# Four of nine parts of a wide projection as block products in a stage of their own

## The chip, the cores and the metric

One core of a Trainium2 chip runs the kernel. The metric is the device time of one execution in microseconds (us); the time of a kernel is the median of several runs. TensorE (PE) multiplies matrices into PSUM; VectorE (DVE), ScalarE (ACT) and GpSimd (POOL) work on data in SBUF, the first two in PSUM too; SyncE (SP) issues most of the transfers.

## The reference: what is computed

One step of a decoder layer for 1024 prompt rows and 8 x 4 sample rows, so T = 1056 rows of 1024 numbers in fp32. Shortened:

```
z = rmsnorm(x, norm_mix_g)
h, c, b, u, v, q, gA, gB, gM = split(z @ w_in)          # nine parts of 1024 columns
y_a = b * causal_dwconv3(c * h)
y_b = u * spatial_gate(layernorm(v))                    # chunks of 128 rows
y_m = softmax(q k_mem^T / 16) v_mem                     # 4 heads, 256 memory rows
x = x + (sig(gA)*y_a + sig(gB)*y_b + sig(gM)*y_m) @ w_o
[a, g] = causal_dwconv3(rmsnorm(x) @ w_up) + bias       # 2 x 2816 columns
y = rmsnorm(x + (silu(g) * a) @ w_down)
```

The prompt attends to memory keys and values that are computed here; each of the 8 sample groups attends to a cache of its own. Outputs are y, the last rows of both convolutions, the memory keys and values, and the normalised v of the sample rows.

## The kernel before

Numbers are held transposed: a tile has 128 of the 1024 features on its partitions and the 1056 rows along it. Every fp32 operand is split into a high part (a rounded copy, on ACT) and a low part (the rest, on DVE or POOL), and every product is three matmuls: high x high, high x low, low x high (`three`, lines 210 to 213). zhi and zlo hold the two parts of the normalised input; S (8 tiles) holds sums.

**Units, chunks and slots.** A unit is one tile of 128 output columns of a weight: 512 KB are loaded by SP into a ring of three buffers (`load_unit`, L166), split into wh and wl (`split_unit`, L188 and L190) up to two units ahead, and used by `main` in three chunks of 352 rows. A chunk is 24 matmuls of 352 columns into one of three PSUM banks ("mm"), and then its evacuation. Side work lies as closures in the list `aux`; `weave` is called twice in each chunk (a slot, half a chunk), and spreads the list evenly over the slots that `pace(n)` announced; `drain` issues what is left. All engines work in the order in which this program issues, each in its own queue.

**Stages.** The part v (24 units) with the norm of x; the memory keys and values; then four heads h of attention, each with 16 units: q (two tiles), h, c, b, h, c, b, u, u, gB, gB, gA, gA, gM, gM. Then w_o, the up projection, the down projection. The first head's evacuations begin at about 190 us, the last gM's are at about 1013; the up projection begins at about 1113.

**A head's side work** (`att_items`, 83 items, and 4 for transposing cached rows) begins behind the two q units and is paced over 62 slots. Item 0 (`rows`) writes the sample rows' q to DRAM; `fetch_q` reads it back spread over all partitions, 512 KB each of eight times; `fetch` loads the sample groups' keys. `product(bb, mt)`, 16 items, is four DVE instructions each (L844), the sample rows' scores. `kv_load` and `kv_split` (ACT, then DVE at L960) bring the prompt's keys and values in two parts; `kv_split` stands between the products of bb = 6 and bb = 7. Then come, interleaved, `score(i)` (12 matmuls, maximum at L978, exponentials at L981, scaling at L988), `turn_p(i)` (transposes of the result and its two parts) and `value(i)` (12 matmuls), i from 0 to 3; then the sample rows' softmax, the values' fetches, their two parts (`parts`) and their matmuls (`against`).

**Evacuations.** q on ACT and DVE (two parts); u multiplies S on DVE (L1125); gB: sigmoid on ACT (L1130) into one of two tiles `sig`, a multiplication into S on DVE (L1136); gA and gM: sigmoid, then two DVE operations (L1143, L1144); h a copy; c a product and the three taps of the convolution (L305, L307); b a product. The last gM also makes zhi and zlo of S for w_o, and S is then loaded anew with x from DRAM.

**Block products.** The up projection already uses Winograd's form of Strassen's scheme: for two tiles of columns (a pair), the input is cut into 2 x 2 blocks of (4 feature tiles) x (two quarters of 264 rows), and seven products in the order 1, 2, 6, 5, 7, 3, 4 replace eight. Sums of input blocks are made once (`norm2`, L1245 to L1250), sums of weight blocks for each pair on POOL (L1361 to L1363, L1384), each sum gets its two parts (L1380, L1381) four products ahead, and the results are added on DVE into a scratch tile and the outputs (`evacuate`, L1477; L1479 on ACT). A product is 24 matmuls of 264 columns into one of three pairs of PSUM banks. The taps of the convolution follow on DVE (L1436, L1440), and the gate's multiplication on POOL (L1453).

**Buffers.** 9 slots for fp32 (`fs`) and 8 for the rounded type (`rs`), each 128 x 1088, are handed out first in, first out.

Of the kernel before, what the change touches and what calls it, by code (L numbers as in the profile page):

```python
# [15 lines left out]
P = 128  # L16
# [41 lines left out]
def layer_step(ctx: ExitStack, tc: tile.TileContext, I, O):  # L58
# [83 lines left out]
    for h in range(4):  # L142
        f0, f1 = 2 * h, 2 * h + 1
        seq = [("q", f0), ("q", f1)]
        for f in (f0, f1):
            seq += [("h", f), ("c", f), ("b", f)]
        for n in ("u", "gB", "gA", "gM"):
            seq += [(n, f0), (n, f1)]
        plan.append(seq)
        for n, f in seq:  # L150
            if (n, f) == ("gM", 7):
                for x in range(4, 8):
                    unit_cols(w_o, x * P, hold=True)
            unit_cols(w_in, COLS[n] + f * P)
    for f in range(8):
        unit_cols(w_o, f % 4 * P)
# [20 lines left out]
    def split_unit(eng=nc.vector):  # L177
        i = state["split"]
        if i < len(units):
            _, nk, cols, hold = units[i]  # L180
            t = stage.pop(i)
            if hold:
                kept[i] = rs.get(), rs.get()
# [4 lines left out]
            nc.scalar.copy(out=hi, in_=t)  # L188
            split_lows()
            lows.append(lambda: eng.tensor_tensor(out=lo, in0=t, in1=f32(hi), op=ALU.subtract))  # L190
            split[i] = (hi, lo)
            state["split"] += 1
# [163 lines left out]
    with tc.manual_schedule():  # L356
        slots = ctx.enter_context(tc.tile_pool(name="slots", bufs=1))
        fs = Slots(slots, [f"fs{i}" for i in range(9)], F32)
        rs = Slots(slots, [f"rs{i}" for i in range(8)], F32R)
# [133 lines left out]
        mh = [rs.get(), rs.get()]  # L493
        ml = [rs.get(), rs.get()]
# [16 lines left out]
        wt = rs.get()  # L511
# [87 lines left out]
        def sgu_norm(j):  # L599
# [13 lines left out]
            def go_n():  # L613
# [14 lines left out]
                for half in range(2):  # L628
                    fr = slice(half * 512, (half + 1) * 512)
                    p = rs.get()  # L630
# [14 lines left out]
        def sgu_mix(j, g):  # L645
            def go():
# [19 lines left out]
                if g % 2:  # L666
                    rs.put(sg.pop(("p", j, g // 2)))
            return go

        def sgu_done():  # L670
            rs.put(wt)
# [134 lines left out]
        rs.put(*mh, *ml)  # L806
# [6 lines left out]
        def att_items(h):  # L813
            qh, ql = att["q"]
            att["ym"] = ym = [None, None]
# [4 lines left out]
            def rows():  # L820
# [3 lines left out]
                att["qr"] = qr = small.tile([P, 256], F32, name="qr", tag="qr", bufs=1)  # L824
                nc.scalar.copy(out=qr[:32], in_=b[:32, :256])
                nc.scalar.dma_start(out=q_d[h], in_=qr[:32])
# [10 lines left out]
            def product(bb, mt):  # L837

                def go():
                    t = v3(att["st", bb // 2], 4, 256)  # L840
                    q = v3(att["qb", bb], 4, 256)
                    for i in range(4):
                        at = 4 * bb + i
                        nc.vector.tensor_tensor_reduce(  # L844
                            out=att["qr"], in0=q[:, i, :], in1=t[:, 2 * (bb % 2) + mt, :], scale=1.0, scalar=0.0,
                            op0=ALU.mult, op1=ALU.add, accum_out=att["sc"][:, mt, at : at + 1],
                        )
                    if mt:
                        fs.put(att.pop(("qb", bb)))
                        if bb % 2:  # L850
                            fs.put(att.pop(("st", bb // 2)))
                return go
# [16 lines left out]
            def masked():  # L869
                att["m"] = [rs.get(), rs.get()]  # L870
# [13 lines left out]
            def parts(i, e):  # L884
                def go():
                    t = att["st", i][:, e * 512 : (e + 1) * 512]
                    k = rs.get()
# [7 lines left out]
            def against(bb):  # L895
                def go():
# [12 lines left out]
                    rs.put(k)  # L909
# [23 lines left out]
            def folded_o():  # L933
# [10 lines left out]
                rs.put(*att.pop("m"))  # L944
# [11 lines left out]
            def kv_split():  # L956
                t = att.pop("kvs")
                hi, lo = rs.get(), rs.get()
# [5 lines left out]
            def score(i):  # L964
                def go():
# [23 lines left out]
                    att["p", i] = p  # L989
                return go  # L990

            def turn_p(i):
                def go():
# [9 lines left out]
                    t = rs.get()  # L1003
# [5 lines left out]
            def value(i):  # L1009
                def go():  # L1010
# [10 lines left out]
                    rs.put(t)  # L1021
                    for dt in range(2):
                        nc.scalar.copy(out=ym[dt][:, i * 256 : (i + 1) * 256], in_=b[:, dt * 256 : (dt + 1) * 256])
                    if i == 3:
                        rs.put(*att.pop("kv"))
# [26 lines left out]
        wo, back = {}, set()  # L1052
        pr = O["new_conv_a_prompt"][0, 0]
        sa = O["new_conv_a_sample"][0].rearrange("b k c -> (b k) c")

        def wo_take(f):
            def go():
                wo[f] = next_unit()
                ahead()
# [3 lines left out]
        def wo_ready(c):  # L1063
            def x_back():
                back.add(c)
                for fr in (slice(0, 4), slice(4, 8)):
                    nc.scalar.dma_start(out=S[:, fr, c * CH : (c + 1) * CH], in_=xT_d[c, :, fr, :])

            aux.extend([lambda: None] * 2 + [x_back])
            pace(3)  # L1070
            if c == 2:
                aux.extend(lambda i=i: tail_rows(tail_a[i // 4], i, 4, pr, sa) for i in (0, 4))
                pace(6)

        for h in range(4):
            qh, ql = [rs.get(), rs.get()], [rs.get(), rs.get()]
            hold = {}
            att["qs"] = small.tile([P, 2, 32], F32, name="qs", tag="qs", bufs=2)

            def q_evac(f):  # L1080
                dc = f % 2

                def go(c, r, ps):
                    if c == 2:
                        nc.scalar.mul(out=att["qs"][:, dc, :], in_=ps[:, CH - 32 :], mul=0.0625)
                    nc.scalar.mul(out=qh[dc][:, r], in_=ps, mul=0.0625)
                    nc.vector.scalar_tensor_tensor(
                        out=ql[dc][:, r], in0=ps, scalar=0.0625, in1=f32(qh[dc][:, r]), op0=ALU.mult, op1=ALU.subtract
                    )
                return go  # L1090

            def h_evac(f):
                hold["h", f] = fs.get()

                def go(c, r, ps):
                    nc.scalar.copy(out=hold["h", f][:, r], in_=ps)
                return go

            def c_evac(f):
                hb, hf = fs.get(), hold["h", f]  # L1100
                halo(hb, hal_a[:, f, :])

                def go(c, r, ps):
                    srcs = hb_parts(c, hb, ps)
                    hs = hf[:, r]
                    hsrc = [hs] if c < 2 else [
                        hs[:, : NP - 2 * CH], hs[:, NP - 2 * CH :].rearrange("p (b x) -> p b x", x=4)
                    ]
                    for (dst, src), hx in zip(srcs, hsrc):
                        nc.vector.tensor_tensor(out=dst, in0=src, in1=hx, op=ALU.mult)  # L1110
                    conv(c, hb, hf, CA + f, 8)
                    if c == 2:
                        tails(hb, tail_a[f // 4], f % 4)
                        fs.put(hb)
                return go

            def b_evac(f):
                def go(c, r, ps):
                    t = hold["h", f]
                    nc.vector.tensor_tensor(out=t[:, r], in0=ps, in1=t[:, r], op=ALU.mult)  # L1120
                return go

            def u_evac(f):
                def go(c, r, ps):
                    nc.vector.tensor_tensor(out=S[:, f, r], in0=ps, in1=S[:, f, r], op=ALU.mult)  # L1125
                return go

            def sig(ps):
                t = small.tile([P, CH], F32, name="sig", tag="sig", bufs=2)
                nc.scalar.activation(out=t, in_=ps, func=AF.Sigmoid)  # L1130
                return t

            def gB_evac(f):
                def go(c, r, ps):
                    t = sig(ps)
                    nc.vector.tensor_tensor(out=S[:, f, r], in0=S[:, f, r], in1=t, op=ALU.mult)  # L1136
                return go

            def add_evac(f, get, done):
                def go(c, r, ps):  # L1140
                    t = sig(ps)
                    src = get()
                    nc.vector.tensor_tensor(out=t, in0=t, in1=src[:, r], op=ALU.mult)  # L1143
                    nc.vector.tensor_tensor(out=S[:, f, r], in0=S[:, f, r], in1=t, op=ALU.add)  # L1144
                    if c == 2:
                        fs.put(src)
                    if done:
                        for half in range(2):
                            fr = slice(4 * half, 4 * half + 4)
                            nc.scalar.copy(out=zhi[:, fr, r], in_=S[:, fr, r])  # L1150
                            nc.vector.tensor_tensor(
                                out=zlo[:, fr, r], in0=S[:, fr, r], in1=f32(zhi[:, fr, r]), op=ALU.subtract
                            )
                        done(c)
                return go

            for i, (n, f) in enumerate(plan[h]):
                if i == 2:
                    att["q"] = (qh, ql)
                    att["f"] = f  # L1160
                    items = att_items(h)
                    if h:
                        items[-6:-6] = [x[0] for x in hals[2 * h - 1 : 2 * h + 1]]
                        items += [x[1] for x in hals[2 * h - 1 : 2 * h + 1]]
                    aux.extend(items)
                    pace(62)
                if n == "u" and h == 0:
                    until(lambda: sg.get("done"))
                if n == "gM":
                    drain()  # L1170
                    if f % 2 == 0:
# [737 lines left out]
```

## Time and profile before

| | |
|---|---|
| median of 3 runs | 1865.82 us (1863.99 to 1866.83) |
| profiled execution | 1862.66 us, span 1860.9 us |
| PE busy | 1825.4 us, 98% |
| DVE busy | 1159.0 us, 62% |
| ACT busy | 637.5 us, 34% |
| POOL busy | 362.6 us, 19% |

How to read it: each engine's busy time is a sum over the span, and engines overlap. In a group line stand the line of the kernel, engine, operation, out<-in, shapes and count, then the busy time and the mean of one in ns, then the idle time in front and what ended it. A timeline line has the start and the duration in us, the engine, line and operation, and in brackets the idle time before and its cause. A windows line has the length, the busy time and count for PE, PE's weight loads, DVE, ACT and POOL, then the granted TensorE clock (1.00 is full), the share of the DMA engines and GB/s. The page rounds and overlaps: a matmul's listed duration is about twice its pitch, since matmuls are pipelined.

### The profile page before, as it was taken

The page shows a single profiled execution, that of the slowest core. Times are in us where ns is not written, and L with a number is a line of the kernel's source. Part 1 is how long each engine was busy: PE and PEld are TensorE (multiplying, and loading weights), DVE is VectorE, ACT ScalarE, POOL GpSimd, SP SyncE. Part 2 cuts the span into 40 slices and gives each one's busy share as a digit, 9 for nine tenths or more (in the row PEclk, how much of TensorE's full clock was granted, in tenths as well). Part 3 has the DMA queues.
Part 4 walks back from the last instruction along what each step waited for, and adds up shares of the span by engine and source line. Part 5 has one row for each costly group of instructions (what it writes and reads, how often), then busy time and mean ns, then how long its engine had stood idle before and what let it go on. Part 6 is the DMA issues. An engine that isn't in the chain of part 4 may idle for free. (4 is left out here: it accounts for less than half of the span.)

```text
span 1860.9 us, 31015 instructions
## 1 busy us (share of the span) xinstructions
PE 1825.4 (98%) x12576; PEld 1798.7 (97%) x12576; DVE 1159.0 (62%) x2146; ACT 637.5 (34%) x1038; POOL 362.6 (19%) x463
## 2 busy tenths in 40 slices
PE   8999999999999999999999998999999999999997
PEld 8998999999999999999999998999999999899997
DVE  4567677336733384327636479888988898655443
ACT  6645312321232113221224233343334334444332
POOL 2231100000000000000000223666566654100000
PEclk9999999999999999999999999999999999999999
DMA  8735253114311432125214431232223222776652
GB/s 259 212 118 185 98 162 103 53 48 162 102 49 46 137 102 83 45 65 175 60 56 126 152 93 40 75 94 74 77 72 92 74 76 99 229 258 222 200 157 91
DMA packets 250091, 215.03 MB, mean 116 GB/s; under 512 B 7893, under 2 KB 235389, under 8 KB 249949
## 3 DMA queue, kind: packets, MB, share of 16 engines
q1 hardware_dynamic: 240036, 199.49, 34.6%
q10 hardware_dynamic: 9913, 13.57, 2.1%
q8 instruction: 99, 1.62, 0.3%
q14 instruction: 43, 0.35, 0.1%
HBM read 183.22 MB, written 29.81 MB: 114 GB/s over the span
## 5 line engine op out<-in xcount | busy, mean ns | idle before, releaser
L211 PE MATMUL mm<-zhi,wh 128*128 128x352 f32 x1728 | 560.9, 325 | 0.3 <-ACT zhi L273 0.3
L212 PE MATMUL mm<-zlo,wh 128*128 128x352 f32 x1728 | 558.1, 323 | 1.1 <-POOL zlo L284 1.0
L213 PE MATMUL mm<-zhi,wl 128*128 128x352 f32 x1728 | 557.7, 323 | 0.2 <-DVE wl L190 0.2
L190 DVE TENSOR_TENSOR wl<-ws,wh 128x1024 fp32r<-128x1024 f32 x183 | 223.3, 1221 | 215.4 <-ACT wh L188 214.3
L211 PE MATMUL pair<-zhi,wh 128*128 128x264 f32 (+1 forms) x1096 | 325.2, 297 | 4.7 <-DVE fs L1477 2.0
L212 PEld LDWEIGHTS mm<-zlo,wh 128*128 128x128 f32 x1728 | 324.5, 188 | 2.4 <-POOL zlo L284 1.9
L211 PEld LDWEIGHTS mm<-zhi,wh 128*128 128x128 f32 x1728 | 325.1, 188 | 1.1 <-ACT zhi L273 0.6
L213 PEld LDWEIGHTS mm<-zhi,wl 128*128 128x128 f32 x1728 | 324.6, 188 | 0.5 <-DVE wl L190 0.5
L212 PE MATMUL pair<-zlo,wh 128*128 128x264 f32 (+1 forms) x1096 | 321.9, 294 | 1.1 <-DVE zlo L1630 1.0
L188 ACT CAST wh<-ws 128x1024 fp32r<-128x1024 f32 (+1 forms) x184 | 187.3, 1020 | 256.3 <-PE mm L212 112.2
L211 PEld LDWEIGHTS pair<-zhi,wh 128*128 128x128 f32 x1096 | 206.1, 188 | 8.6 <-issue 4.2
L212 PEld LDWEIGHTS pair<-zlo,wh 128*128 128x128 f32 x1096 | 206.5, 188 | 1.6 <-DVE zlo L1630 1.6
L213 PE MATMUL pair<-zhi,wh 128*128 128x264 f32 x704 | 200.1, 284 | 0.0
L211 PE MATMUL pair<-fs,wh 128*128 128x264 f32 (+1 forms) x506 | 151.4, 299 | 0.4 <-DVE rs L1477 0.2
L212 PE MATMUL pair<-fs,wh 128*128 128x264 f32 (+1 forms) x506 | 150.4, 297 | 1.0 <-DVE fs L1630 1.0
L213 PEld LDWEIGHTS pair<-zhi,wh 128*128 128x128 f32 x704 | 132.6, 188 | 0.0
L213 PE MATMUL pair<-zhi,wl 128*128 128x352 f32 (+1 forms) x392 | 121.6, 310 | 1.4 <-DVE wl L190 1.4
L844 DVE CUSTOM_DVE_ANT_0 qr<-fs,fs 128x256 f32<-128x256 f32 x256 | 108.4, 424 | 7.3
L213 PE MATMUL pair<-fs,wh 128*128 128x264 f32 x344 | 98.0, 285 | 0.0
L1130 ACT ACTIVATE sig<-mm 128x352 f32<-128x352 f32 x72 | 33.4, 464 | 187.9 <-PE mm L213 187.5
L212 PEld LDWEIGHTS pair<-fs,wh 128*128 128x128 f32 x506 | 95.3, 188 | 1.2 <-DVE fs L1630 1.2
L211 PEld LDWEIGHTS pair<-fs,wh 128*128 128x128 f32 x506 | 95.4, 188 | 0.8 <-issue 0.8
(330 smaller groups left out, 3117.3 us busy)
## 6 DMA issues: line engine op xcount, KB each, us to landing
ws<-in_w_in SPq DMA_DIRECT2D x88, 512.0 KB
ws<-in_w_down SPq DMA_DIRECT2D x60, 512.0 KB
fs<-q_d SPq DMA_DIRECT2D x32, 512.0 KB
ws<-in_w_up SPq DMA_DIRECT2D x46, 256.0 KB
S<-in_w_up SPq DMA_DIRECT2D x42, 256.0 KB
fs<-in_cache_mem_k SPq DMA_DIRECT2D x16, 512.0 KB
fs<-in_cache_mem_v SPq DMA_DIRECT2D x16, 512.0 KB
rs<-act_d SPq DMA_DIRECT2D x14, 528.0 KB
```

What stands on the lines that cost most here:

```text
L188: nc.scalar.copy(out=hi, in_=t)
L190: lows.append(lambda: eng.tensor_tensor(out=lo, in0=t, in1=f32(hi), op=ALU.subtract))
L211: mmul(ps, lhsT=wh, rhs=xh, start=first, stop=False)
L212: mmul(ps, lhsT=wh, rhs=xl, start=False, stop=False)
L213: mmul(ps, lhsT=wl, rhs=xh, start=False, stop=last)
L844: nc.vector.tensor_tensor_reduce(out=att["qr"], in0=q[:, i, :], in1=t[:, 2 * (bb % 2) + mt, :], scale=1.0, scalar=0.0, op0=ALU.mult, op1=A ...
L1130: nc.scalar.activation(out=t, in_=ps, func=AF.Sigmoid)
```

## The change

- The parts h, c, b and gA (32 of the 64 units) leave the heads. They become 16 pairs of block products behind the heads, by the scheme of the up projection: for each pair of tiles first h, then c, b, gA. zhi and zlo serve as four of the seven input forms; the other three (6, 7, 4) are made in new slots by `b_forms` beside gB7, gM6 and gM7, and form 5 over zhi and zlo when the stage has begun.
- The other parts come in six groups: q0 | u0 B0 u1 B1 q1 | M0 u2 q2 | M1 B2 q3 | M2 u3 B3 | M3 (B is gB, M is gM, and the number is the pair of tiles). Head h's side work is woven into group h + 1, over 58, 34, 34 and 30 slots.
- u's first two tiles are kept aside until the spatial gate has finished S.
- S now collects gB and gM first, gA last. Parts of S for w_o and the reload of x (now on SP) are woven into the last pair, and w_o's four held units are taken within the w_o stage.
- One pool of 17 slots serves both types. The PSUM pairs are opened before the new stage.

The diff, cut to its core:

```diff
-    for h in range(4):
...
-        seq = [("q", f0), ("q", f1)]
-        for f in (f0, f1):
-            seq += [("h", f), ("c", f), ("b", f)]
-        for n in ("u", "gB", "gA", "gM"):
-            seq += [(n, f0), (n, f1)]
+    for names in ("q0", "u0 B0 u1 B1 q1", "M0 u2 q2", "M1 B2 q3", "M2 u3 B3", "M3"):
...
-        fs = Slots(slots, [f"fs{i}" for i in range(9)], F32)
-        rs = Slots(slots, [f"rs{i}" for i in range(8)], F32R)
+        fs = Slots(slots, [f"fs{i}" for i in range(17)], F32)
...
+        def b_forms(s):
...
+            return [
+                whole("a", 0, s + 2), whole("b", 0, s), whole("c", 1, s + 2),
+                minus("b", "a", "b"), minus("a", "c", "a"), parts(7, "a", True),
+                minus("c", "c", "b"), whole("d", 1, s), parts(6, "c", False),
+                free_c, parts(4, "d", True), last,
+            ]
...
+        def b_sums(e):
...
+                tt = nc.gpsimd.tensor_tensor
+                tt(out=s1, in0=a21, in1=a22, op=ALU.add)
+                tt(out=s2, in0=s1, in1=a11, op=ALU.subtract)
+                tt(out=a21, in0=a11, in1=a21, op=ALU.subtract)
...
+        def b_prepare():
...
+                nc.scalar.copy(out=hi, in_=a)
+                nc.vector.tensor_tensor(out=lo, in0=a, in1=f32(hi), op=ALU.subtract)
+                bwf[e, n] = hi, lo
+                if n == 1:
+                    nc.gpsimd.tensor_tensor(out=a, in0=braw[e][2], in1=braw[e][6], op=ALU.subtract)
+                elif n == 3:
+                    b_load(e + 1, 1)
+                elif n == 4:
+                    braw.pop(e)
+                    b_load(e + 2, 0)
+                    b_sums(e + 1)
...
+        def b_out(e, half, c, ps, x):
...
+            t = gates()
+            tt(out=t.rearrange("p (s t) -> p s t", t=QC), in0=ps, in1=x, op=ALU.add)
+            if n == "c":
+                to = hbs[f][:, 2 + c * QC : 2 + (c + 2) * QC]
+                tt(out=to, in0=to, in1=t, op=ALU.mult)
+                if (half, c) in ((0, 2), (1, 0)):
+                    late.extend(conv_a_items(f))
+            elif n == "b":
+                tt(out=outs[f][:, r], in0=outs[f][:, r], in1=t, op=ALU.mult)
...
+        for i, seq in enumerate(plan):
+            h = i - 1
+            if 0 <= h < 4:
+                drain() if h else None
+                items = att_items(h)
...
+                aux.extend(items)
+                pace(6 * len(seq) - 2 if h < 3 else 30)
...
+                if (n, f) == ("gB", 7):
+                    drain()
+                    aux.extend(b_forms(0))
+                    pace(6)
+                if (n, f) == ("gM", 6):
+                    aux.extend([lambda: (b_load(0, 0), b_load(0, 1), b_load(1, 0))] + b_forms(1))
+                    aux.extend([lambda: b_sums(0)] + [b_prepare] * 4)
+                    pace(12)
...
+        for e, n in bsteps:
+            b_prepare()
...
+            for s in range(2):
+                xh, xl = bform[n, s]
+                for k in range(4):
+                    three(ps[:, s, :QC], wh[:, k, :], wl[:, k, :], xh[:, k, :], xl[:, k, :], k == 0, k == 3)
+            b_evacuate(e, n, ps)
...
+        for i in range(4, 8):
+            at_point(i, 1, lambda: ahead(4))
```

`whole` adds zhi and zlo of a block on POOL (1056 numbers a partition), `minus` subtracts two such on DVE, `parts` makes the two parts on ACT and DVE. `b_evacuate` is the up projection's `evacuate` with `b_out` for the outputs; `conv_a_items` is its `conv_items` (one ACT operation, two taps on DVE) without bias.

More of the change, by code (lines that the diff above doesn't have):

```diff
@@ L805, in layer_step @@
         drain()
[L806 removed]
+        fs.put(*mh, *ml)
         aux.extend(sgu)
@@ L1049, in att_items @@
             return items
[L1052 to L1059, printed above, removed]
-            return go
[L1063 to L1171, printed above, removed]
-                        rs.put(*qh, *ql)
-                    if f == 6:
-                        aux.extend(wo_take(x) for x in range(4, 8))
-                        pace(5)
-                if n == "gA":
-                    ev = add_evac(f, lambda f=f: hold["h", f], None)
-                elif n == "gM":
-                    ev = add_evac(f, lambda f=f: att["ym"][f % 2], wo_ready if f == 7 else None)
-                else:
-                    ev = {"q": q_evac, "h": h_evac, "c": c_evac, "b": b_evac, "u": u_evac, "gB": gB_evac}[n](f)
-                main(ev)
@@ new lines, in layer_step, with to_parts, x_back @@
+        drain()
+        psums.close()
+        pools["pair"] = ctx.enter_context(tc.tile_pool(name="psp", bufs=3, space=bass.MemoryType.PSUM))
+        pools["aux"] = ctx.enter_context(tc.tile_pool(name="psb", bufs=2, space=bass.MemoryType.PSUM))
+        bslot["u"] = fs.get()
+        def to_parts(fr, r, eng=nc.vector):
+            nc.scalar.copy(out=zhi[:, fr, r], in_=S[:, fr, r])
+            eng.tensor_tensor(out=zlo[:, fr, r], in0=S[:, fr, r], in1=f32(zhi[:, fr, r]), op=ALU.subtract)
+        def x_back(fr):
+            for c in range(3):
+                nc.sync.dma_start(out=S[:, fr, c * CH : (c + 1) * CH], in_=xT_d[c, :, fr, :])
@@ new lines, in layer_step @@
+        for e, n in bsteps:
+            b_prepare()
+            for _ in range(2 if n == 1 else 1):
+                if late:
+                    late.popleft()()
+            wh, wl = bwf.pop((e, n))
+            ps = pair()
+            for s in range(2):
[3 more added lines that the diff above has]
+            b_evacuate(e, n, ps)
+            if e == 0 and n in (1, 2):
+                b_form5(n - 1)
+            if e == len(bpairs) - 1:
+                if n == 3:
+                    late.popleft()()
+                for go in b_end.get(n, ()):
+                    go()
+                if n == 3:
+                    to_parts(slice(6, 7), right)
+                if n in (6, 7, 4):
+                    for s in range(2):
+                        fs.put(*bslot.pop((n, s)))
```

304 lines of the change are left out of this document (259 added, 45 removed).

## The prediction

> **What bounds the kernel now.** I read the busy line of the page first, then the windows over the span, then single engines' timelines inside a head and inside the up projection.
>
> ```profile
> PE 1825.4 (98%) x12576; PEld 1798.7 (97%) x12576; DVE 1159.0 (62%) x2146; ACT 637.5 (34%) x1038; POOL 362.6 (19%) x463
> ```
> ```profile
> 300.00:350.00 50.00, 50.00 (x346) 49.65 (x345) 23.65 (x54) 19.67 (x48) 1.91 (x2) 1.00 0.25 75
> 400.00:450.00 50.00, 50.00 (x315) 49.92 (x314) 19.26 (x50) 9.95 (x18) 0.00 (x0) 1.00 0.39 128
> 450.00:500.00 50.00, 50.00 (x326) 49.96 (x325) 41.96 (x144) 10.57 (x23) 1.95 (x6) 1.00 0.34 106
> 1300.00:1350.00 50.00, 50.00 (x411) 49.89 (x410) 45.45 (x61) 17.18 (x26) 27.21 (x37) 1.00 0.26 77
> ```
>
> TensorE never idles in the heads (300 to 500) or in the up projection (1300 to 1350), so both stages cost what their matmuls cost. VectorE is uneven: 19 us of 50 in most of a head, but 42 of 50 where the score products of the sample rows lie (450 to 500). That peak is covered today because a head has 14 units of projection to spread its side work over. Busy time does not give the price of a matmul; starts do:
>
> ```profile
> 428.67 0.45 ACT L1096 COPY fs<-mm 128x352 f32<-128x352 f32 x1 [1.55 <-PE mm L213]
> 432.52 0.45 ACT L1096 COPY fs<-mm 128x352 f32<-128x352 f32 x1 [3.39 <-PE mm L213]
> ...
> 1277.08 2.28 POOL L1363 TENSOR_TENSOR S<-ws,S 128x512 f32<-128x512 f32 x1
> 1297.78 2.28 POOL L1363 TENSOR_TENSOR S<-ws,S 128x512 f32<-128x512 f32 x1
> ```
>
> A chunk (24 matmuls of 352 columns) takes 3.85 us: its evacuations follow at that pitch. A pair of tiles by seven block products (168 matmuls of 264) takes 20.70 us: the once-a-pair sum L1363 repeats at that pitch.
>
> **The change, part by part.**
>
> *Block products: the gain.* Out go 32 units of h, c, b, gA: 96 chunks x 3.85 = 369.6 us (with the pitch of 3.85, rounded). In come 16 pairs x 20.70 = 331.2. Gain 38.4 us, if TensorE stays the bound there. Is VectorE able to keep up? Its work in a pair:
>
> ```profile
> L1477 DVE TENSOR_TENSOR rs<-pair,S 128x528 f32<-128x528 f32 x70 | 48.8, 697 | 0.0
> L1381 DVE TENSOR_TENSOR wh<-S,wh 128x512 fp32r<-128x512 f32 x85 | 61.8, 727 | 16.3 <-ACT wh L1380 16.3
> L1436 DVE SCALAR_TENSOR_TENSOR rs<-rs,vec,rs 128x1024 f32<-128x1024 f32 x52 | 80.9, 1556 | 0.0
> L1440 DVE SCALAR_TENSOR_TENSOR rs<-ext,vec,rs 128x32 f32<-128x32 f32 x64 | 34.2, 534 | 0.0
> ```
>
> Each pair has 7 sums (0.70) and 7 low parts (0.73): 10.0 us. The heaviest, b, has the taps of two tiles as well (4 x 1.56 + 4 x 0.53 = 8.4) and four multiplications of the sums' size (2.8): 21.2 us against 20.70; its neighbours have 10 to 16. Four prepared forms and three PSUM pairs cover such a half-microsecond, so I count nothing; without that cover it costs 0.5 us on each of four pairs. The second weight tile of a pair is loaded one step later than in the up projection, and three sums on POOL follow it, still two steps ahead of their use: nothing.
>
> *Attention beside fewer units: the cost.* Heads 1, 2 and 3 get 6 units each (36 half-chunk slots), where they had 14. The side list has 87 items with the halo items; it is paced over 34 slots (30 for head 3), so 2.56 items a slot (2.9), against 1.4 before. The score products are 16 of the items numbered 8 to 43, then score(0) is item 45; kv_split, which makes the high and low parts that score(0) multiplies, is item 40.
>
> ```profile
> 446.75 0.41 DVE L844 CUSTOM_DVE_ANT_0 qr<-fs,fs 128x256 f32<-128x256 f32 x1
> 448.61 0.42 DVE L844 CUSTOM_DVE_ANT_0 qr<-fs,fs 128x256 f32<-128x256 f32 x1
> ...
> 485.47 1.23 DVE L960 TENSOR_TENSOR rs<-fs,rs 128x1024 fp32r<-128x1024 f32 x1
> ...
> 491.68 0.68 DVE L978 TENSOR_REDUCE mx<-aux 128x2 f32<-128x512 f32 x1
> 493.65 0.62 DVE L988 TENSOR_SCALAR fs<-fs,sm 128x256 f32<-128x256 f32 x2
> ```
> ```profile
> L190 DVE TENSOR_TENSOR wl<-ws,wh 128x1024 fp32r<-128x1024 f32 x183 | 223.3, 1221 | 215.4 <-ACT wh L188 214.3
> L1130 ACT ACTIVATE sig<-mm 128x352 f32<-128x352 f32 x72 | 33.4, 464 | 187.9 <-PE mm L213 187.5 <-DVE wl L190 0.3
> L1143 DVE TENSOR_TENSOR sig<-sig,fs 128x352 f32<-128x352 f32 x48 | 25.2, 526 | 107.9 <-ACT sig L1130 107.9
> L1125 DVE TENSOR_TENSOR S<-mm,S 128x352 f32<-128x352 f32 x24 | 12.5, 521 | 34.0 <-PE mm L213 34.0
> ```
>
> An item of four products takes 1.86 us. Head 1, from its first slot (units M0, then u): item 8 is reached in slot 4, behind the evacuation of the second chunk: 2 x 3.85 + 0.46 (sigmoid) + 2 x 0.53 = 9.2 us. VectorE then has in order, up to and with kv_split: 14 items x 1.86 = 26.0, four gM evacuations of two operations 4.2, two low parts of weights 2.4, two u evacuations 1.0, kv_split 1.2: together 34.8, so it ends at 44.0. TensorE runs ahead (the sigmoids empty PSUM, and three banks hold chunks) and comes to score(0) after nine chunks, 34.7 us. It must wait 9.3 us. Head 2 has the same numbers (M1, then gB evacuations of the same length). Head 3, at 2.9 items a slot, comes to score(0) after eight chunks, 30.8 us, with one u evacuation fewer on VectorE: 43.5, a wait of 12.7. Sum 31.3. Queued behind the waiting matmuls is the whole projection; behind kv_split on VectorE are two more items (3.7 us) and then the maximum for score(0). The stretch from that maximum to the scaled result is 2.6 us (491.68 to 494.27), and turn_p(0) stands one slot (1.9 us) and one score product behind, so it waits about 2 us more in each head: 6.
>
> *The clock.* The three waits are long enough for another price:
>
> ```profile
> 1158.07 0.36 PE L211 MATMUL pair<-rs,wh 128*128 128x264 f32 x1 [3.77 <-DVE fs L1477]
> ...
> 1159.49 0.42 PE L212 MATMUL pair<-rs,wh 128*128 128x264 f32 x1
> 1159.71 0.42 PE L213 MATMUL pair<-rs,wh 128*128 128x264 f32 x1
> ```
> ```profile
> 1155.00:1160.00 5.00, 1.93 (x10) 1.96 (x11) 4.60 (x5) 2.81 (x4) 3.08 (x6) 0.84 0.00 0
> 1160.00:1165.00 5.00, 4.75 (x31) 4.29 (x31) 4.30 (x10) 2.25 (x2) 1.30 (x1) 0.82 0.71 210
> ```
>
> After an idle stretch of 3.77 us the matmuls started 0.22 us apart instead of 0.12, and the granted clock (the third column from the end) was 0.84 and 0.82 in the two windows of 5 us: 0.16 x 5 + 0.18 x 5 = 1.7 us lost. In a head it falls together with the wait for turn_p(0) and is within the 2 us. The Trainium skill (TensorE: Matmul & The Clock Gate, part 1, the clock gate) says that the gate works in free-running windows of 3.4 us, cold after one idle window and warm only after one busy one; by that a restart early in a window could stay cold for almost two, and my sum would be up to 1.7 us larger in each of four places. The one case in this trace shows a single window, and I go by it.
>
> *Exponentials among sigmoids.* Before, a head had its exponentials together and one switch each way. Now gB chunks stand beside the scores of heads 0 and 2, and a switch lies at almost every one: about eight more.
>
> ```profile
> 534.45 1.28 ACT L1130 ACT_TABLE_LOAD   x1
> 535.75 0.47 ACT L1130 ACTIVATE sig<-mm 128x352 f32<-128x352 f32 x1
> ```
>
> Eight of 1.28 us are 10 us of a ScalarE that is a third busy; part falls in the chain from score to turn_p. I put 2 us on the path, bounds 0 and 10. The Trainium skill (ScalarE: Activation LUTs, What ACT_TABLE_LOAD costs) adds a drain of about 1.38 us to each load, 2.66 in all, which would make my 2 into 4; here the sigmoid started right behind the load, so the measurement decides.
>
> *Head 0 and second halves.* Head 0 keeps its pace (105 items in 58 slots against 62) with lighter evacuations: about 1 us. The value fetches have 6 items, or 2.3 slots, to land, where they had over 4; about 1 us, bounds 0 and 6.
>
> *Forms of the input, before the stage.* Two sets are woven into gB7, gM6 and gM7:
>
> ```profile
> L1453 POOL TENSOR_TENSOR rs<-rs,rs 128x1056 f32<-128x1056 f32 x10 | 28.3, 2827 | 10.9 <-ACT S L1452 10.9
> L1250 DVE TENSOR_TENSOR S<-S 128x1056 f32<-128x1056 f32 x8 | 11.0, 1371 | 0.1
> L1245 ACT CAST zhi<-S 128x1056 fp32r<-128x1056 f32 x8 | 8.6, 1074 | 5.3 <-DVE S L1256 5.3
> L1246 DVE TENSOR_TENSOR zlo<-S,zhi 128x1056 fp32r<-128x1056 f32 x8 | 10.6, 1326 | 2.0 <-ACT zhi L1245 2.0
> ```
>
> A set is four POOL sums (2.83), four differences (1.37) and three splits (1.07 on ScalarE, then 1.33). VectorE stands for two sums (1.9 + 5.7 = 7.6 us into gB7), then for the third, and has the first set done, with gB7's evacuations, at about 21.6, where gB7 ends on TensorE at 11.5. The second set (4 x 1.37 + 3 x 2.4 = 12.7), one low part 1.2, five gM evacuations 5.3 and the first prepared form bring it to about 41; TensorE is through gM7 at 34.7 (nine chunks). It waits some 6 us, plus 1.7 for the clock: 7.7, bounds 2 (ScalarE and VectorE work overlaps fully) and 12.
>
> *Moved, at nothing.* Four held units of w_o are split in the w_o stage instead of in gM7: 4 x 1.22 on VectorE over eight steps of about 3 us, which is its spare time there. Their loads stand on SP behind the reload of x, which waits for the last splits; the fourth unit is first used six steps (18 us) later. If that cover is gone, about 3 us. The merged pool frees slots at the same items; no term.
>
> *Sum.* -38.4 + 31.3 + 6 + 2 + 2 + 7.7 = +10.6. The profiled execution took 1862.66 us (span 1860.9), so 1873.3. The median of the timed runs is 3.2 above the profiled one: 1876 us.
>
> **Rivals.** *The waits swallow each other (faster).* Place: behind score(0). If the time that TensorE loses there lets VectorE work off its queue, turn_p, the fetches and the forms find their inputs ready, the 17.7 us of secondary terms vanish and the gain of 38.4 meets 31.3: 1859 us. For it: a stalled TensorE gives everything else time. Against it: kv_split is followed by 3.7 us of products on the same queue, and the forms come a head later. It decides where all waits together are under 38 us, which with my secondary terms is an average of 7 at score(0). Should the products also be reached earlier or run shorter than I count, it goes down to 1850.
>
> *A wash.* All waits come to 35 to 42 us; the time stays within 0.2% (3.7 us, about what a measurement of this kernel can tell).
>
> *The new stage is not bound by TensorE (still slower).* VectorE's 21.2 us in b, and POOL's sums late behind a load, cost 2 to 3 us on half of the pairs: some 20 us on top, 1896. For it: the chain of the up projection runs through POOL's sums. Against it: that stage has more VectorE work and its pitch is even.
>
> *The change does not do what it says:* the sums of blocks could cost more instructions than counted; but the code has 16 x 7 products of 24 matmuls, 2688 for 2304, so the 12% fewer columns are certain.
>
> **How the numbers follow.** Forecast (1870 to 1890) 0.52; swallowed waits (1850 to 1862) 0.27; wash 0.13; stage not bound by TensorE 0.08. The range from 1852 to 1890 leaves out the last case and the tail of the second. The likeliest case alone: 1870 to 1890. Faster by over 0.2%: 0.27; within: 0.13; slower: 0.60.
>
> **What would show it.** In the changed profile: TensorE waits of 8 to 13 us for L960's low part, three times, with granted clock under 1 behind each; VectorE full from the third to the ninth chunk of each short head; a wait of about 6 us ahead of the first block product; 20.5 to 20.9 us a pair afterwards, TensorE busy throughout. It is wrong if the pairs' pitch is not near 20.7, or if the waits in the heads sum to less than 30 us.

## The result, and the profile after

The changed kernel is slower: 1887.35 us (median of 4 runs, 1886.49 to 1887.99) against 1864.9 for the kernel before (4 runs, 1862.94 to 1866.83), a ratio of 1.012 with a 95% interval of 1.0103 to 1.0138. The forecast was slower by 10; it is slower by 22. The profiled execution took 1886.49 us (span 1884.8), 23.9 more in the span than before.

The page's busy line, then the groups of waits of TensorE (what waited, for what, us in total, times, longest):

```profile
PE 1803.8 (96%) x12960; PEld 1774.1 (94%) x12960; DVE 1303.6 (69%) x2246; ACT 694.2 (37%) x1133; POOL 489.8 (26%) x545
```
```profile
PE aux L969 <- DVE fs L955: 27.4, 3, 11.5
PE pair L205 <- DVE fs L1687: 6.2, 3, 3.8
PE pair L205 <- ACT zhi L1348: 6.0, 2, 3.6
PE pair L205 <- ACT sig L1072: 5.0, 1, 5.0
PE acc L897 <- DVE fs L884: 4.1, 4, 2.1
PE pair L207 <- DVE wh L1205: 2.4, 1, 2.4
```

TensorE is busy for 22 us less and yet the span is longer. The first group is the wait at score(0) (kv_split's low part, L955 here), three times; the second is in the up projection and was there before. The others are new: the start of the block stage (L1072, L1205), its end (L1348), the sample rows' weights (L884).

Windows around the three scores, then around the stage's end (columns as in the prediction; the granted clock is the third from the end):

```profile
375.00:400.00 25.00, 17.03 (x103) 16.78 (x103) 23.72 (x95) 3.75 (x5) 0.00 (x0) 0.90 0.28 88
475.00:500.00 25.00, 17.02 (x103) 16.77 (x102) 23.75 (x94) 5.01 (x7) 0.00 (x0) 0.88 0.27 85
575.00:600.00 25.00, 13.50 (x80) 13.25 (x79) 23.68 (x95) 3.73 (x4) 0.00 (x0) 0.79 0.32 101
```
```profile
1015.00:1020.00 5.00, 2.23 (x19) 2.02 (x17) 3.78 (x4) 1.16 (x2) 2.44 (x1) 0.98 0.34 98
1020.00:1025.00 5.00, 4.17 (x19) 4.20 (x20) 4.33 (x6) 3.44 (x3) 0.00 (x0) 0.50 0.74 241
1025.00:1030.00 5.00, 5.00 (x37) 5.00 (x37) 3.97 (x6) 1.58 (x2) 0.00 (x0) 0.84 0.79 258
1030.00:1035.00 5.00, 1.47 (x9) 0.95 (x8) 4.22 (x7) 2.77 (x4) 0.00 (x0) 0.84 0.28 103
1035.00:1040.00 5.00, 4.98 (x22) 4.98 (x23) 3.56 (x6) 1.63 (x3) 0.00 (x0) 0.50 0.50 147
```

In the first three VectorE is busy for 23.7 of 25 us and TensorE for 13.5 to 17.0: there the bound has changed hands. In the last five neither is full. TensorE waits 3.6 us before the sixth product of the last pair, then 2.4 and 1.2 us at w_o's first product, and behind each place runs a stretch at half clock.

The new stage itself, one line of its first evacuation (16 copies, first and last start):

```profile
L1291 ACT COPY fs<-pair x16: 592/601/602, 699.5 to 1005.5; 128x528 f32<-128x528 f32 x16
```

That is 306.0 us for 15 pairs, 20.40 a pair: the change does what it says, and 16 pairs cost 326.4 us where 96 chunks cost 369.6.

### The profile page after: what moved, and what is told of

Read it like the earlier page. It is cut to its first block, busy times and chain, and to the rows that moved or that the text cites. A ratio compares the mean times of both kernels' runs of the same rounds, so it can differ in the third digit from the quotient of the medians.

```text
span 1884.8 us, 32215 instructions
## 1 busy us (share of the span) xinstructions
PE 1803.8 (96%) x12960; PEld 1774.1 (94%) x12960; DVE 1303.6 (69%) x2246; ACT 694.2 (37%) x1133; POOL 489.8 (26%) x545
## 4 chain that ended last, share of the span: by engine, by line
PE 57%; DVE 17%; issue 10%; POOL 9%; ACT 3%; DMA 2%; ACTq 0%; SPq 0%; DVEq 0%; POOLq 0%
PE pair L206 11%; PE pair L207 11%; PE pair L205 11%; PE mm L205 5%; PE mm L207 5%; PE mm L206 5%; DVE fs L837 4%; POOL fs L1663 2%; DVE wl L184 2%; POOL S L1575 2%; DVE fs L1646 1%; POOL S L1574 1%; POOL ws L1596 1%; POOL S L1573 1%; DVE wh L1593 1%
## 5 line engine op out<-in xcount | busy, mean ns | idle before, releaser
L205 PE MATMUL pair<-zhi,wh 128*128 128x264 f32 (+1 forms) x1608 | 474.9, 295 | 15.3 <-ACT zhi L1348 6.0
L206 PE MATMUL pair<-zlo,wh 128*128 128x264 f32 (+1 forms) x1608 | 471.6, 293 | 1.9 <-DVE zlo L1349 1.2
L205 PE MATMUL pair<-fs,wh 128*128 128x264 f32 (+1 forms) x1124 | 330.9, 294 | 4.7 <-DVE fs L1687 4.1
L206 PE MATMUL pair<-fs,wh 128*128 128x264 f32 (+1 forms) x1124 | 327.7, 292 | 0.7 <-DVE fs L1460 0.7
L205 PEld LDWEIGHTS pair<-zhi,wh 128*128 128x128 f32 x1608 | 306.9, 191 | 20.0 <-ACT zhi L1348 6.4
L205 PE MATMUL mm<-zhi,wh 128*128 128x352 f32 x960 | 315.4, 329 | 0.3 <-ACT zhi L267 0.3
L206 PE MATMUL mm<-zlo,wh 128*128 128x352 f32 x960 | 312.0, 325 | 1.0 <-POOL zlo L278 1.0
L207 PE MATMUL mm<-zhi,wl 128*128 128x352 f32 x960 | 311.1, 324 | 0.2 <-DVE wl L184 0.2
L184 DVE TENSOR_TENSOR wl<-ws,wh 128x1024 fp32r<-128x1024 f32 (+1 forms) x151 | 187.4, 1243 | 163.4 <-ACT wh L182 162.8
L207 PE MATMUL pair<-fs,wh 128*128 128x264 f32 x904 | 256.2, 283 | 0.0
L207 PEld LDWEIGHTS pair<-zhi,wh 128*128 128x128 f32 x1216 | 231.1, 190 | 2.7 <-DVE wh L1205 2.7
L205 PEld LDWEIGHTS pair<-fs,wh 128*128 128x128 f32 x1124 | 212.1, 189 | 5.8 <-ACT fs L1629 4.0
L206 PEld LDWEIGHTS pair<-fs,wh 128*128 128x128 f32 x1124 | 212.2, 189 | 0.9 <-DVE fs L1460 0.9
L207 PEld LDWEIGHTS pair<-fs,wh 128*128 128x128 f32 x904 | 170.4, 188 | 0.0
```

What stands on the lines that cost most here:

```text
L205: mmul(ps, lhsT=wh, rhs=xh, start=first, stop=False)
L206: mmul(ps, lhsT=wh, rhs=xl, start=False, stop=False)
L207: mmul(ps, lhsT=wl, rhs=xh, start=False, stop=last)
```

## The experiments

Twelve kernels ran, each compared with the kernel before in the same series (1863.5 to 1863.9 us). Differences below are to the changed kernel's 1887.35. The kernel before moves by up to 1.4 us from series to series, and single executions of kernels that are alike up to the start of the stage reach it up to 2.6 us apart, so a median's difference says little under 2 us, and a place in one trace nothing under 3 us.

My theory at the outset: at score(0) TensorE waits out a backlog of VectorE's, and each wait brings half clock. The rival: the attention's data (transfers) come late, so lighter VectorE work would change nothing.

### Is it VectorE's backlog at score(0)?

**few_products** computes only one of the four score products of each item in heads 1 to 3, with all transfers kept.

```diff
-                    for i in range(4):
+                    for i in range(1 if h else 4):
```

> Heads 1 to 3 compute one of each four sample-row products (the other scores are left at zero); all transfers, kv_split and everything else stay as in the changed kernel. Theory (VectorE's backlog of products makes TensorE wait at score(0)): the three waits for the keys' low part (27.4 us in all) fall under 2 us, the half clock behind them (about 6.7 us lost) goes too, and the time falls from 1887 to 1850 to 1858. Rival (the fetches of half a MB each are late on SP): the waits stay at 20 us or more, the time at 1878 or more.

1854.56 us, ratio 0.9949 (0.9934 to 0.9964), 32.8 less. Its longest waits:

```profile
PE pair L205 <- DVE fs L1689: 6.2, 3, 3.8
PE pair L205 <- ACT zhi L1350: 5.9, 2, 3.6
PE pair L205 <- ACT sig L1074: 5.4, 1, 5.4
PE acc L899 <- DVE fs L886: 4.1, 4, 2.1
```
```profile
L1293 ACT COPY fs<-pair x16: 592/603/603, 666.1 to 972.2; 128x528 f32<-128x528 f32 x16
```

The three waits of 27.4 us are gone and the other four groups are as they were. The stage starts 33.4 us sooner (666.1 against 699.5), which is the whole difference. So the three waits came from VectorE's queue and not from the transfers, which all stayed; and the rest of the loss lies elsewhere, since it stayed too.

**kv_early** moves kv_load and kv_split ahead of the score products.

```diff
+                items[3], items[7] = kv_load, kv_split
...
-                    items += [kv_load, started]
+                    items += [started] if early else [kv_load, started]
```

> In heads 1 to 3 kv_load and kv_split stand ahead of the products instead of between the last two. Theory (the backlog): the maximum for score(0) still stands behind all 16 products on VectorE, so the wait only moves from the keys' low part to turn_p(0), is as long, and the time stays at 1882 to 1892. Rival (kv_split is merely placed too late): the waits vanish, 1850 to 1860.

1886.78 us, ratio 1.0126 (1.0109 to 1.0143): no change. The wait has only changed its line:

```profile
PE aux L995 <- DVE fs L983: 32.8, 4, 12.1
```

score(0) now runs at once, and turn_p(0) waits for a maximum and a scaling (L983) that stand behind the same products. It is the length of the queue that counts, not what is at its head.

### Can another order hide it?

**mixed_order** puts the prompt's items between the products from bb = 2 on, heads 1 to 3.

```diff
+                        items.append(product(bb, mt))
+                        if bb > 1:
+                            items.append(prompt.pop(0))
```

> In heads 1 to 3 the twelve items of the prompt's attention stand between the products of bb = 2 to 7 in place of the empty items, behind an early kv_split. Theory (the backlog; VectorE has 2.9 us of work a slot there against 2.9 us on TensorE when they are mixed): TensorE's waits in heads 1 to 3 fall from 27.4 to under 6 us with at most one half-clock stretch, and the time to 1850 to 1862. Rival (a head's VectorE work is too much for six units whatever its order): the waits come back at turn_p or at the values' parts, 1875 or more.

1889.84 us, ratio 1.014 (1.0125 to 1.0155): a miss; the time is the rival's. The waits spread out instead:

```profile
PE aux L969 <- DVE fs L955: 11.6, 3, 4.4
PE aux L852 <- DVE sc L837: 6.5, 6, 1.8
PE aux L968 <- ACT fs L954: 3.0, 2, 1.5
```

**mix2** starts with kv_split before the first product, interleaves from the second product on with empty places between an item and the one that needs it, and puts the softmax of the sample rows behind the first two `parts`.

```diff
+                items += [rows, kv_load, fetch(kc, 0), fetch(kc, 1), fetch_q(0), fetch_q(1), kv_split]
...
+                        if bb or mt:
+                            items.append(prompt.pop(0))
```

> In heads 1 to 3 the splits of keys and values stand before the sample-row products, the groups of the input projection stand between the products from the first one on, and each softmax stands two units of TensorE work behind its scores. Backlog theory (the head's waits come from VectorE's queue being longer than the TensorE work put beside it, and can be covered by putting that work nearer): the 27.4 us of waits at the heads fall to 8 or less, the half clock behind them goes, and the time is 1865 to 1875. Rival (VectorE has more to do in these heads than six units of TensorE work last, whatever the order): the waits spread over other lines, their sum stays above 20 us, and the time is 1882 or more.

1870.29 us, ratio 1.0033 (1.0021 to 1.0045), 17.1 less. The time is in the expected range, but the waits are not under the 8 us that were expected. The longest ones left there:

```profile
PE aux L206 <- DVE fs L1002: 7.7, 5, 1.9
PE acc L897 <- DVE fs L923: 5.8, 4, 3.1
PE aux L995 <- DVE fs L983: 2.5, 2, 1.5
PE aux L969 <- DVE fs L955: 1.5, 2, 0.8
```

With the smaller ones the waits of heads 1 to 3 come to 19.3 us, the longest 3.1, against 32.7 in the changed kernel (27.4 at score(0), 5.3 at the sample rows' weights); and the granted clock over 350 to 650 us is 0.98 against 0.95. The rival of mix2 (too much for six units in any order) falls: about half of the 33 us that few_products won in the heads was order. The other half may still be too much work; no run tells.

### What does the clock cost behind these waits?

**warm** fills the three waits with matmuls that nothing reads (44, 44 and 64, ahead of score(0)).

```diff
+                    if i == 0 and h:
+                        w = bank("acc")[:, :CH]
+                        for _ in range((0, 44, 44, 64)[h]):
+                            mmul(w, lhsT=zhi[:, 0, :P], rhs=zhi[:, 0, :CH], start=True, stop=True)
```

> Adds 44, 44 and 64 matmuls of 352 columns on TensorE alone (into a bank that the next step overwrites; nothing reads them) ahead of the first scores of heads 1, 2 and 3, so that TensorE works while it would have waited there. Clock theory (the stretches at half clock behind these three waits, 13.4 us of busy time, cost about 6.7 us): they vanish, the waits become work, and the time is 1879 to 1882. Rival (TensorE has time to spare behind these waits, so the half clock costs nothing there): 1886 to 1889.

1888.2 us, ratio 1.0126 (1.0111 to 1.0141): no change, so my clock theory missed and the rival held. TensorE's timeline at the first score in the changed kernel, then in warm, then two groups of warm's waits:

```profile
397.98 0.58 PE L969 MATMUL aux<-fs,fs 128*128 128x256 f32 x1 [7.97 <-DVE fs L955]
398.36 0.42 PE L970 MATMUL aux<-fs,fs 128*128 128x256 f32 x1
398.57 0.41 PE L968 MATMUL aux<-fs,fs 128*128 128x256 f32 x1
398.79 0.41 PE L969 MATMUL aux<-fs,fs 128*128 128x256 f32 x1
```
```profile
399.26 0.28 PE L972 MATMUL aux<-fs,fs 128*128 128x256 f32 x1
399.38 0.28 PE L973 MATMUL aux<-fs,fs 128*128 128x256 f32 x1
```
```profile
PE aux L999 <- DVE fs L987: 4.7, 4, 1.2
PE aux L973 <- DVE fs L955: 3.1, 3, 1.3
```

In warm the scores run at full clock, 0.12 us apart instead of 0.21, and TensorE then waits 4.7 us at turn_p in four waits (L999; in the changed kernel the same line, L995, waits 1.0 us, once). VectorE still sets the pace there, so a fast TensorE only arrives early. In these three places, where TensorE is not the bound, half clock costs nothing.

### The block stage's two ends

**fdve** makes the sums of the forms on VectorE.

```diff
-                    nc.gpsimd.tensor_tensor(
+                    nc.vector.tensor_tensor(
                         out=as4(t[n]), in0=f32(block(zhi, h, c)), in1=f32(block(zlo, h, c)), op=ALU.add
```

> The sums of the block products' forms are made on VectorE instead of GpSimd. Theory (a GpSimd instruction of 11.9 us at 630.6 holds VectorE's work beside it up, and the product with the weights waits 4.1 us and runs at half clock behind that): that wait and the half clock at 637 go, 1882 to 1885. Rival (VectorE is full there and the sums only lengthen its queue): the wait ahead of the first block product grows by 2 us or more, 1887 or more.

1882.03 us, ratio 1.0098 (1.008 to 1.0115), 5.3 less. Timelines of VectorE and GpSimd in the changed kernel, then of VectorE in fdve:

```profile
630.48 0.68 DVE L884 TENSOR_TENSOR fs<-fs,fs 128x512 fp32r<-128x512 f32 x1
631.08 3.51 DVE L184 TENSOR_TENSOR wl<-ws,wh 128x1024 fp32r<-128x1024 f32 x1
634.51 2.94 DVE L884 TENSOR_TENSOR fs<-fs,fs 128x512 fp32r<-128x512 f32 x1
```
```profile
630.56 11.87 POOL L1133 TENSOR_TENSOR fs<-zhi,zlo 128x1056 f32<-128x1056 f32 x4 [18.93 <-DVE S L1077]
```
```profile
634.26 1.22 DVE L184 TENSOR_TENSOR wl<-ws,wh 128x1024 fp32r<-128x1024 f32 x1
635.39 0.69 DVE L884 TENSOR_TENSOR fs<-fs,fs 128x512 fp32r<-128x512 f32 x1
```

Beside GpSimd's sums the same two instructions take 3.51 and 2.94 us, without them 1.22 and 0.69. The waits at the sample rows' weights (4.1 us for L884) fall to 0.7. Here eight VectorE sums more are cheaper than standing behind GpSimd. The Trainium skill (SBUF — State Buffer, Who interferes with whom) gives a reason: the two engines share a pair of ports under an exclusive lock, and a VectorE instruction with two inputs in SBUF contends with a GpSimd instruction that reads SBUF. These rows agree.

**flate** makes forms 6 and 4 of the second set inside the first block products, and the others sooner.

```diff
-                    aux.extend([lambda: b_sums(0)] + [b_prepare] * 4)
+                    aux.extend([lambda: b_sums(0), x[4], b_prepare, x[6], x[7], b_prepare, x[11], x[5]] + [b_prepare] * 2)
+                    b_later = [x[8], lambda: (x[9](), x[10]())]
```

> Two of the seven forms of the second set of weights are made inside the first block products instead of ahead of the stage, and the others are made earlier. Theory (TensorE waits 5.0 and 2.4 us ahead of the first block products for forms that queue on VectorE and ScalarE, and runs 4.8 us at half clock behind that): both waits fall below 2 us, 1878 to 1882. Rival (the late forms make a later block product wait as long): the same waits at another product, 1886 to 1889.

1880.77 us, ratio 1.0085 (1.007 to 1.01), 6.6 less. Of 5.0 and 2.4 us in front of the first products 0.6 remains; a new wait of 1.7 us stands in the first pair, a small part of what the rival said:

```profile
688.26 0.39 PE L205 MATMUL pair<-zhi,wh 128*128 128x264 f32 x1 [0.55 <-ACT sig L1072]
704.83 0.39 PE L205 MATMUL pair<-zhi,wh 128*128 128x264 f32 x1 [1.73 <-DVE fs L1289]
```

**end_on_dve** makes the low parts of the attention's sum at the end of the stage on VectorE instead of GpSimd.

```diff
-            1: [lambda: to_parts(slice(0, 4), left, nc.gpsimd)],
-            2: [units_o, lambda: to_parts(slice(4, 6), left, nc.gpsimd)],
+            1: [lambda: to_parts(slice(0, 4), left)],
+            2: [units_o, lambda: to_parts(slice(4, 6), left)],
```

> The two low parts of S that the last pair gives to POOL (2112 and 1056 numbers a partition) are made on VectorE instead. Theory (while POOL's subtraction of 4.75 us ran, a VectorE operation of 0.69 us took 4.82, so POOL held it up): VectorE gets back about 6 us of blocked time for 3.6 us of work, the waits of TensorE at the end of the new stage (3.6, 2.4 and 1.2 us, and about 5.9 us of half clock) fall by half or more, 1877 to 1883. Rival (the last pair is too full on ScalarE and VectorE, whoever subtracts): the same waits, 1885 to 1891.

1885.5 us, ratio 1.0117 (1.0102 to 1.0132), only 1.9 less, a miss: the time is the rival's. The cause that I saw was real. In the changed kernel (GpSimd, then VectorE):

```profile
1008.08 4.75 POOL L1349 TENSOR_TENSOR zlo<-S,zhi 128x2112 fp32r<-128x2112 f32 x1 [9.86 <-PE pair L207]
```
```profile
1004.59 0.68 DVE L1205 TENSOR_TENSOR wh<-ws,wh 128x512 fp32r<-128x512 f32 x1
1008.55 4.82 DVE L1205 TENSOR_TENSOR wh<-ws,wh 128x512 fp32r<-128x512 f32 x1 [3.28 <-ACT wh L1204]
```

0.68 us became 4.82. With GpSimd out of it, VectorE's operation is short again and the wait before the sixth product (3.6 us) is gone. But the wait at w_o's first product has grown from 2.4 to 4.1 us. TensorE, then ScalarE in end_on_dve:

```profile
1032.39 0.39 PE L205 MATMUL pair<-zhi,wh 128*128 128x264 f32 x1 [4.10 <-ACT zhi L1348]
```
```profile
1030.73 0.64 ACT L1276 ACTIVATE sig<-sig 128x528 f32<-128x528 f32 x1 [3.27 <-DVE sig L1267]
```

TensorE waits for a split of S (L1348) that stands behind a sigmoid on ScalarE, and the sigmoid waits for an addition (L1267) in VectorE's queue. So GpSimd's hold explains the first wait and not the second, and TensorE loses here a part of what it won before the sixth product: from the last L1291 copy to the up projection it takes 126.7 us, against 130.4 in the changed kernel.

**end2** reorders that end on the changed kernel: additions ahead of splits, the right half's splits ahead of the left's, nothing on GpSimd.

```diff
+            1: [cp(slice(0, 4), left)],
+            2: [units_o, cp(slice(4, 6), left), sub(slice(0, 2), left)],
+            6: [],
+            5: [sub(slice(2, 4), left), cp(slice(0, 4), right), split_unit],
```

> The changed kernel with only the end of the block stage reordered on VectorE as in all5. Theory: 13 us are lost at that end (7.2 of waits and about 6 of half clock); the wait before the last pair's sixth product goes, some 2 us of waits at the output projection's first steps stay, 1877 to 1882. Rival (VectorE has too much to do there in any order): 1884 to 1887.

1885.63 us (1881.93 to 1886.77), ratio 1.0109 (1.0093 to 1.0125): a miss; the time is the rival's. The wait before the sixth product is gone; these remain, all in w_o, the first at its first product (with 1.2 us more for the low part), the other two at its sums of squares:

```profile
PE pair L205 <- ACT zhi L1348: 2.3, 1, 2.3
PE aux L1442 <- DVE fs L1536: 2.9, 2, 1.5
```

From the last L1291 copy to the first copy of the up projection it takes 127.5 us, against 130.4 in the changed kernel; without any wait, 17.5 for six products, 99.5 for w_o as before and 1.7 for the first product make 118.7. So 11.7 us are lost at this end in the changed kernel and the reorder wins 2.9, no more than single traces scatter; the rest is lost again in w_o's first steps and its sums of squares, and in cold clock behind those.

### Everything together

**all3** is mix2, fdve, flate and end_on_dve in one kernel.

> The edits of the runs mix2, fdve, flate and end_on_dve together. Theory (four places, each with a wait and a cold stretch of its own): the four differences to the changed kernel, -17.1, -5.3, -6.6 and -1.9 us, add to -30.9, so 1856.5, faster than the kernel before. Rival (all of them are one queue on VectorE, and what is taken out at one place comes back at the next): less than half of the small three remains, 1864 or more.

1858.25 us, ratio 0.997 (0.9959 to 0.9981): 29.1 of the 30.9 us, and 5 us faster than the kernel before (1863.5 in its series). The four places are nearly independent.

```profile
PE 1796.6 (97%) x12960; PEld 1765.8 (95%) x12960; DVE 1296.2 (70%) x2256; ACT 716.5 (39%) x1151; POOL 461.6 (25%) x535
```
```profile
PE aux L206 <- DVE fs L1002: 7.8, 5, 1.9
PE acc L897 <- DVE fs L923: 5.3, 3, 3.1
PE pair L205 <- ACT zhi L1374: 4.1, 1, 4.1
```

**all4** adds one more item between turn_p and value, and one before the first `against`.

```diff
-                prompt = [score(0), score(1), no, turn_p(0), score(2), turn_p(1), value(0), score(3), value(1), turn_p(2)]
...
+                prompt = [score(0), score(1), no, turn_p(0), score(2), turn_p(1), score(3), value(0), turn_p(2), value(1)]
...
```

> As all3, with one more unit of TensorE work between the transposes of the probabilities and the product with the values, and between the masked softmax and the product with the weights. Theory: the 7.7 us (five waits up to 1.9) and the 5.8 us (four, up to 3.1) that the run mix2 still waits there fall to about half, 4 to 7 us less than all3. Rival: VectorE's queue is the limit there and the waits move to the neighbours, no change from all3 within 2 us.

1856.83 us, ratio 0.9963 (0.9951 to 0.9976), not told apart from all3. The 7.8 us fell to 2.0, and a new group took its place, as the rival said:

```profile
PE aux L852 <- DVE sc L837: 7.4, 6, 1.5
```

**all5** is all3 with end2's order.

> As all3 with the end of the block stage put in another order on VectorE: the evacuations of the last pair's products stand ahead of the splits of the attention's output, the right half's splits ahead of the left's, and none of them on GpSimd. Theory (TensorE waits at the end because the evacuation that frees its bank is queued behind splits and late sums): the 4.1 us wait before the last pair's sixth product and the half clock behind it go, 5 to 8 us less than all3. Rival (too much work for VectorE there in any order): the wait moves into the output projection's first steps, no gain within 2 us.

1858.24 us, ratio 0.9967 (0.9955 to 0.998): no gain over all3, as its rival said.

## Why the prediction was right in direction and short in size

From the first q evacuation to w_o's first product the kernel before takes 822.1 us (190.4 to 1012.5). 64 units at 3 x 3.85 are 739.2 of it, so the attention's matmuls are 82.9. Without any loss the changed kernel's 32 units and the same attention would bring the stage to 190.4 + 369.6 + 82.9 = 642.9; it starts at 691.26. These 48.4 us, and what follows, by the prediction's steps:

| step | forecast | measured | from |
|---|---|---|---|
| block products | -38.4 | -43.2 | 16 x 20.40 - 369.6 |
| score(0) and turn_p, clock within | 31.3 + 6 | 33.4 | few_products |
| tables, head 0, fetches | 2 + 2 | 4.7 | 48.4 - 33.4 - 5.0 - 5.3, not tested by itself |
| forms, start of the stage | 7.7 | 10.1 | 5.0 waited, then 8.2 for a first product of 3.1 |
| sums on POOL beside the last head | 0 | 5.3 | fdve |
| end of the stage | 0 | 11.7 | 130.4 - 118.7 |
| behind w_o | 0 | 1.7 | rest of the span |
| sum | 10.6 | 23.7 | the spans differ by 23.9 |

The rows are known to some 3 us, since most come from single traces; fdve's 5.3 is a difference of medians (its trace reaches the stage 3.7 sooner). That the miss is not larger is luck in part: the two terms that I had too dear, the products and the heads, take off 8.7 us.

**Heads: right.** Three waits of 8, 8 and 11.5 us at score(0), where I worked out 9.3, 9.3 and 12.7; VectorE nearly full; the cold clock behind them cost nothing of its own, as said, and warm shows it. Tables: 14 loads stand at the sigmoid (L1072) and exponential (L976) lines, against 8 before, and one at the sample rows' exponentials: seven more where I had eight. With head 0 and the fetches they have the 4.7 us that the other rows leave.

**The gain: a little larger.** I took 20.70 us a pair from the up projection; the new stage runs at 20.40. Why it is shorter was not tested. VectorE's 21.2 us in b did not show.

**The failing step is "Moved, at nothing".** I named a cover (eight steps of w_o with spare VectorE time) and a price of 3 us if it were gone, and looked only at w_o's weights. To what the change also weaves into the last pair, the splits of S for w_o, I gave no term. Two of them take 4.75 and 2.44 us on GpSimd; on VectorE (end_on_dve) all but the last take 9.2. They stand beside 17.5 us of matmuls in which VectorE also empties PSUM and makes the late sums. TensorE waits 7.2 us and runs a cold stretch behind each place, and in place of nothing the end costs 11.7 us, most of a miss of 13. That GpSimd made the first wait is shown by end_on_dve. What would hide the second stays open: VectorE is busy for 19.9 of the 25 us shown, so it is not sheer work; the chain from addition to sigmoid to late sum to split may be what is too long, but neither reorder settles that.

**A term that was missing** is what GpSimd does to VectorE. I counted GpSimd's sums as free work beside VectorE's and VectorE's durations as constant; beside L1133 they trebled (1.22 to 3.51), 5 us on the path.

**The clock: one place too small, one free.** I went by one row, 1.7 us a place. By the same count the five windows at the stage's end lose 0.02 x 5 + 0.5 x 5 + 0.16 x 5 + 0.16 x 5 + 0.5 x 5 = 6.7 us, 3.3 a place. Both counts take in time in which TensorE waited anyway. By the matmuls, 25 and 22 of them start 0.22 us apart instead of 0.12, which is 2.5 and 2.2 us; with the waits of 7.2 that makes 11.9, near the 11.7 of the table. In the row that I went by 13 did, 1.3 us. So a place costs about twice what that row showed, by either count: the granted clock is 0.50 from 1019.8 to 1026.6 us, 6.8 us on end. By the Trainium skill (TensorE: Matmul & The Clock Gate, part 1, the clock gate) the array turns cold after an idle window of some 3.4 us and warm again only after a busy one. This trace agrees with two such windows, which the prediction had named and I had set aside. In the heads the clock cost nothing, by warm.

**The rivals.** Waits did not swallow each other: kv_early shows a backlog that stays whole when its head moves. The stage is bound by TensorE, which is busy for all of 720 to 1000 us. Of what I said would prove me wrong, the pitch (20.40) is near 20.7. The waits at score(0) sum to 27.4, under the 30 that I set; with those at the sample rows' weights the heads have 32.7, but 3.4 of these are GpSimd's doing, by fdve. So the mark is met or not by what one counts, and few_products stands by the mechanism.

## What to carry to other kernels

When side work loses the matmuls that hid it, add up the queue of the engine that does it from the last moment it was empty; the wait will sit wherever the queue first meets TensorE (kv_early), and what helped here was a shorter queue (few_products) or more matmuls put beside it (mix2). Give each edge of a new stage a sum of its own: here the heads were worked out to within 4 us, and the stage's end, at nothing, was most of the miss. And before a cold clock is priced, ask who is the bound behind it; where it is another engine, as in the heads here, the clock costs nothing.

## What the runs showed of the hardware

While GpSimd worked, VectorE's operations grew from 0.68 to 4.82 us and from 1.22 to 3.51. Moving GpSimd's sums to VectorE won 5.3 us, though they lengthen its queue; moving its two splits won 1.9, no more than the noise. Matmuls behind waits of 2.4 to 11.5 us ran at about half pitch (0.21 us instead of 0.12 for 256 columns). At the stage's end 25 and 22 matmuls did so behind a wait, 2.5 and 2.2 us, where the one row in the kernel before has 13. In the heads such stretches cost nothing (1888.2 us without them, 1887.35 with them).
